# Max-pool subtract on one core: tiles of five rows in five slots, a loop by tile, and the last wait on SyncE

## The chip, the cores and the metric

One core of a Trainium2 chip; the other cores are idle. The metric is device time in microseconds (us), the median of several executions. All runs below were in the fast state: the clock that the chip granted, as a share of the full one, was 1.000. The "span" is the time from the first to the last instruction in a profile, some 1.8 us less than the device time. A transfer "lands" when its semaphore tells that all of it has arrived. A "row" is always the kernel's unit of 128 partitions x 8 KB = 1.049 MB. The kernel moves 128 rows in and 128 rows out.

## The reference

```python
# x: float32, B, C, H, W = 8, 64, 256, 256
x_r = x.reshape(B, C, 32, 8, 32, 8)
pooled = x_r.max(axis=(3, 5))
upsampled = np.repeat(np.repeat(pooled, 8, axis=2), 8, axis=3)
return x - upsampled
```

Each 8 x 8 window loses its own maximum. Every byte is read once and written once: 268.44 MB.

## The kernel before

SyncE issues the loads and ScalarE the stores. VectorE takes a tile's maxima in one reduce and subtracts them row by row, in place in the ring. TensorE only relays "loaded" semaphores into one counter. The tiles lie in the slots of a ring in on-chip memory. The first tile (the head) and the last (the tail) are worked in smaller pieces, of the rows that `HEAD` and `TAIL` list.

```python
HEAD = [2, 2]; SIZE = 4; ROUNDS = 5; TAIL = [2, 1, 1]; SLOTS = 6
ring = data.tile([P, SLOTS * SIZE * ROW], F32, name="ring")     # ROW = 2048 floats
# ... SyncE: a slot is loaded again when its store has landed
        if landed[slot]:
            nc.sync.wait_ge(stored[slot], 16 * landed[slot])
        nc.sync.dma_start(out=sbuf(i, lo, R), in_=dram(x_rows, i)[:, part])   # ...
# ... ScalarE
        nc.scalar.wait_ge(ready, done)
        nc.scalar.dma_start(out=dram(out_rows, i)[:, part], in_=sbuf(i, lo, R))   # ...
    nc.scalar.wait_ge(final, 16 * n_final)
# ... VectorE: the head, then
    with nc.vector.Fori(0, ROUNDS):
        with nc.vector.Fori(0, SLOTS) as slot:
            take(filled, 1)
            pool_and_subtract(ring[:, bass.ds(slot * (SIZE * ROW), SIZE * ROW)], ..., SIZE)
# ... then the tail
```

## Time and profile before

| | before |
|---|---|
| device time, first three runs | 627.47 us (627.42 to 627.50) |
| span in the profile | 625.5 us |
| VectorE busy | 562.6 us (90%) |
| the two DMA queues | 49.9% + 49.7% of 16 engines' span |
| period of a four-row tile | 19.36 us |
| last landing to end of span | 1.11 us |

A busy VectorE and a busy set of DMA engines stand side by side here. Which one bounds is read from who waits for whom.

### The profile page before, as it was taken

To read this page: it belongs to the slowest core of one execution; us is meant where nothing else is said; L and a number is where in the kernel's file an instruction comes from. 1 tells how busy PE (TensorE), PEld (TensorE's weight loads), DVE (VectorE), ACT (ScalarE), POOL (GpSimd) and SP (SyncE) were. 2 spreads that over 40 slices of the span, in tenths; PEclk is the share of its full clock that TensorE was granted. 3 is DMA by queue.
4 is the path that set the end of the run, shared out by engine and by line. 5 is a ranking of instruction groups with operands and counts; after the bars stand their busy time and mean duration, and the time that the engine had idled before them with its cause. 6 is when DMAs were issued, how large, how long until landed. Compare 5 with 4: busy or idle time off the path is not lost. (4 is left out here: it accounts for less than half of the span.)

```text
span 625.5 us, 613 instructions
## 1 busy us (share of the span) xinstructions
DVE 562.6 (90%) x163; POOL 0.2 (0%) x4
## 2 busy tenths in 40 slices
DVE  4999999998898888988889888898888998888983
POOL 0000000000000000000000000000000000000000
DMA  8999999999999999999999999999999999999998
GB/s 369 402 434 438 436 434 436 434 436 434 434 432 427 425 434 436 436 436 434 436 434 436 434 434 427 430 425 436 436 436 434 436 436 434 434 436 434 425 427 363
DMA packets 9792, 268.44 MB, mean 429 GB/s; under 512 B 1088, under 2 KB 1088, under 8 KB 1088
## 3 DMA queue, kind: packets, MB, share of 16 engines
q1 hardware_dynamic: 4752, 134.22, 49.9%
q10 hardware_dynamic: 5040, 134.22, 49.7%
HBM read 134.22 MB, written 134.22 MB: 429 GB/s over the span
## 5 line engine op out<-in xcount | busy, mean ns | idle before, releaser
L81 DVE TENSOR_REDUCE tops<-ring (+2 forms) x35 | 278.4, 7953 | 48.4 <-DVEq L75 48.4
L93 DVE TENSOR_TENSOR ring<-ring,tops (+1 forms) x128 | 285.0, 2287 | 5.2 <-DVEq L75 0.2
L164 POOL MEMSET const-bfloat16-1.0<- 128x1 bf16 x1 | 0.1, 102 | 0.0
L164 POOL MEMSET const-uint8-127<- 128x1 uint8 x1 | 0.1, 102 | 0.0
L164 POOL MEMSET const-float32-0.0<- 128x1 f32 x1 | 0.1, 99 | 0.2 <-issue 0.2
L164 POOL MEMSET const-float32-1.0<- 128x1 f32 x1 | 0.1, 99 | 0.0
## 6 DMA issues: line engine op xcount, KB each, us to landing
ring<-in_x_dram SPq DMA_DIRECT2D x31, 4096.0 KB, 62.1
out_dram<-ring ACTq DMA_DIRECT2D x30, 4096.0 KB, 35.9
out_dram<-ring ACTq DMA_DIRECT2D x3, 2048.0 KB, 19.3
ring<-in_x_dram SPq DMA_DIRECT2D x2, 2048.0 KB, 9.5
out_dram<-ring ACTq DMA_DIRECT2D x2, 1024.0 KB, 9.2
```

The lines of the kernel that those rows point to most:

```text
L81: nc.vector.tensor_reduce(out=maxs if R > 1 else maxs[:, 0], in_=(wins.rearrange("p r ph ow pw -> p r ow ph pw") if R > 1 else wins[:, 0]. ...
L93: sub = nc.vector.tensor_tensor(out=wins[:, r], in0=wins[:, r], in1=maxs[:, r].unsqueeze(1).unsqueeze(3).to_broadcast([P, pH, oW, pW]), op ...
L164: nc = _bacc.Bacc("TRN2", target_bir_lowering=False, num_devices=1)
```

## The change

The intent is fewer, larger transfers, a simpler loop and shorter waits around VectorE. The title of the change also names the head "in halves"; the head was `[2, 2]` before, so this changes nothing.

```diff
-HEAD = [2, 2]
-SIZE = 4
-ROUNDS = 5
+HEAD, HEAD_OUT = [2, 2], [2, 2]
+SIZE, TILES = 5, 24
 TAIL = [2, 1, 1]
-SLOTS = 6
+SLOTS = 5
...
-        ).then_inc(reduced, 1)
-        take(reduced, 1)
+        ).then_inc(reduced if nth is None else pooled, 1)   # pooled: head and tail, no decrement
...
-        nc.scalar.wait_ge(final, 16 * n_final)
+        nc.sync.wait_ge(final, 16 * n_final)
...
-        with nc.vector.Fori(0, ROUNDS):
-            with nc.vector.Fori(0, SLOTS) as slot:
-                take(filled, 1)
+        with nc.vector.Fori(0, TILES) as i:
+            slot = i % SLOTS
+            take(filled, 1)
...                                # head and tail wait on the load's semaphore directly
```

## The prediction

> **What bounds the kernel now.** I read the page first, beginning with its busy shares and the row of DMA shares:
>
> ```profile
> span 625.5 us, 613 instructions
> DVE 562.6 (90%) x163; POOL 0.2 (0%) x4
> ...
> DMA  8999999999999999999999999999999999999998
> ...
> DMA packets 9792, 268.44 MB, mean 429 GB/s; under 512 B 1088, under 2 KB 1088, under 8 KB 1088
> ...
> q1 hardware_dynamic: 4752, 134.22, 49.9%
> q10 hardware_dynamic: 5040, 134.22, 49.7%
> ```
>
> VectorE (DVE) works 90% of the span, but the DMA engines have no slice below eight tenths, and the packets of the load queue (q1) and the store queue (q10) fill 49.9% + 49.7% = 99.6% of what 16 engines have. Next the stretches: the first microseconds, the steady middle, the end.
>
> ```profile
> 2.00:3.00 1.00, 0.00 (x0) 0.00 (x0) 1.00 1.02 229
> 3.00:4.00 1.00, 0.00 (x0) 0.00 (x0) 1.00 0.93 393
> ...
> 100.00:590.00 490.00, 447.70 (x128) 0.00 (x0) 1.00 1.00 433
> ...
> 616.00:618.00 2.00, 0.21 (x1) 0.00 (x0) 1.00 1.05 451
> ...
> 620.00:622.00 2.00, 0.00 (x0) 0.00 (x0) 1.00 1.04 438
> ```
>
> The last two columns are DMA share and GB/s. From 100 to 590 us the share is 1.00; after VectorE's last instruction ends at 616.2 us the DMA still runs full until the last packet ends at 624.0 us (packet records). So the set of 16 engines is the bound from the first load to the last store. VectorE only waits for it, in the timeline and the waits:
>
> ```profile
> 539.94 8.69 DVE L81 TENSOR_REDUCE tops<-ring  x1 [1.64 <-DVEq L75]
> 548.78 8.90 DVE L93 TENSOR_TENSOR ring<-ring,tops  x4
> ...
> 559.30 8.69 DVE L81 TENSOR_REDUCE tops<-ring  x1 [1.62 <-DVEq L75]
> ...
> SPq L110 <- DMA out_dram<-ring: 522.6, 26, 47.2
> ```
>
> One tile takes 559.30 - 539.94 = 19.36 us, of which VectorE idles 1.6 us; SyncE (SP) waits for stores in order to reload a slot. Last, the issues:
>
> ```profile
> ring<-in_x_dram SPq DMA_DIRECT2D x31, 4096.0 KB, 62.1
> out_dram<-ring ACTq DMA_DIRECT2D x30, 4096.0 KB, 35.9
> ```
>
> A load lands 62.1 us after its issue, over three periods of 19.36, so some two more loads always stand queued behind it; a store lands after 35.9, so the store queue has a backlog of 35.9 - 19.4 = 16.5 us. Neither queue runs dry.
>
> **A ledger of the DMA time.** A row is one unit of 128 x 8 KB = 1.049 MB; the kernel moves 128 rows in and 128 out. The steady period is 19.362 us for 8 rows (landings of the load semaphores, 116.17 us for six tiles), 2.4203 us a row. 256 x 2.4203 = 619.6 us. The first packet starts at 1.93 us and the last ends at 624.01, which is 622.08, so about 2.5 us are lost besides; the slow first microseconds above (229 and 393 GB/s) are where, because at every later landing the count of rows moved lies the same 2.7 us behind. The remaining 1.9 us before the first packet and 1.5 us after the last are start, receipt and closing barriers.
>
> Of the 2.4203 us, how much hangs on packet size? The packet records have medians of 309 ns for 8192 B, 611 for 16384 and 1213 for 32768: doubling costs 302 and 602, so 7 to 9 ns are fixed. The period says somewhat less: 8 rows at 435.2 GB/s are 19.275 us, the measured excess is 0.087 us for 16 data packets on each engine, 5.4 ns each. So **5 to 8 ns a packet**.
>
> **What the Trainium skill says.** "DMA: Bandwidth & Descriptors", section "Specifications", gives a fabric ceiling of 435 GB/s for a core's 16 DMA engines; the trace agrees, 433 to 435 in the long windows, so there is at most half a per cent above this kernel. The same page, section "Why small descriptors are slow (HBM only)", states a fixed overhead of about 3 cycles per packet; the trace has 5 to 8 ns, more than 3 cycles of the 850 MHz that the page names, but of that kind. Its section "Queues, rings and completion order" says that each DMA engine round-robins between its queue rows at packet granularity. The trace agrees in a way that matters here: while the head is stored in 16 KB packets beside loads in 32 KB packets, stores get a third of the engines. From 36.88 to 51.48 us they moved 2 rows and loads 4. Its section "Latency and other measured facts" warns of HBM row pitches that are large powers of two; the old pitch (32 KB) shows no such loss here, and the new one (40 KB) is not a power of two.
>
> **The change, part by part.**
>
> *Larger tiles.* Thirty tiles of four rows become 24 of five: the loads go from 33 to 27, the stores from 35 to 29. Data packets: before, 7808 of 32 KB, 640 of 16 KB, 256 of 8 KB, in all 8704; after, 24 x 128 x 2 = 6144 of 40 KB, 128 of 32 KB for the last load, the same 640 and 256, in all 7168. That is 1536 fewer, and 12 x 16 = 192 fewer completion packets of 9 ns. Saved: 1536 x 5 to 8 ns / 16 = 0.48 to 0.77 us, plus 192 x 9 / 16 = 0.11 us. **About 0.6 us.** All of this is on the path, because the DMA engines never idle.
>
> *VectorE.* A four-row reduce takes 8.686 us and a two-row one 4.42, so 2.13 a row: five rows 10.82. Five subtractions at 8.90 / 4 = 2.225 are 11.13. With the 0.15 us gap a tile needs 22.1 us against a DMA period of 10 x 2.418 = 24.18, so it still waits about 2 us a tile. Its busy total stays near 562 us. The loop's new remainder (slot from tile number) is one register operation; those of the old loop take 0.05 to 0.1 us and stand between landing and reduce, off the path. The waits taken directly instead of through TensorE's relay, and without the decrement, shorten a landing-to-reduce time of 0.3 us at the head and tail. That is off the path too.
>
> *Five slots.* The ring holds 25 rows instead of 24, but after the head only four tiles, still 24 rows, are loaded ahead. With 40 KB load packets beside 16 KB head stores, stores get 2/7 of the engines: 4 rows stored while 10 are loaded. At 21.2 us, where stores begin, 7.2 rows are loaded; so 17.2 are loaded when the head is out, at 4.6 + 21.2 x 2.42 = 56 us (before: 51.5 us, with 15.5 loaded). From there the queues alternate evenly and loads stay 13.2 rows ahead of stores (before about 11). Then a load waits in line (24 - 17.2 + 5) x 4.84 = 57 us, and a store lands 13.2 x 4.84 - 22.4 = 41 us after its issue. Both exceed the 24.2 us of a transfer; no queue runs dry. The same working gives 62 and 35 for before, which matches the page's 62.1 and 35.9.
>
> *The end.* When the last load lands, some 12 rows are still to be stored, 12 x 2.42 = 29 us. VectorE is done with the second last tile about then and with the last (2, 1 and 1 rows) 19 us later, eight before the last row must be there. So the end is still the draining of the store queue.
>
> *SyncE in place of ScalarE for the last wait.* Before: the last landing at 624.37, ScalarE's branch at 624.39, its drain at 624.54, SyncE's closing instruction at 624.58. After, one hop between engines goes, but SyncE's two closing waits, done early before, come after the last landing; they stand 0.06 us apart. Net 0, give or take 0.1 us.
>
> Sum: 627.47 - 0.6 = **626.9 us**.
>
> **Rivals.** (1) *VectorE becomes the bound*, if five-row tiles run slower than their shape says. For: only 2.1 us a tile of slack. Against: the forms scale evenly from one to two to four rows (2.28, 4.42, 8.69), and the subtractions don't change. A tile at 25 us would make 24 x 0.8 = 19 us more, 646. Very unlikely. (2) *The 40 KB runs are cut into two packets each*, or go slower. Nothing in the profile has one above 32 KB. A cut would make 6144 more packets, up to 6144 x 8 / 16 = 3.1 us more than my count: 629 to 630. Unlikely, and still inside 2%. (3) *Coarser slots starve a queue*: a load can be issued only once five rows are out. Against: the ledger's lines of 57 and 41 us. If it happened once a tile for 1 us, 24 us more. (4) *No gain at all*: the small excess over 435.2 GB/s goes with bytes[...], not packets; then 627.4. This is the strongest rival, since the two ways to get the packet's cost differ by half. (5) *More gain than mine*: were the 9 ns of packet overhead fully serial, 1 us; 626.4.
>
> **Range and chances.** Rivals 4 and 5 give 627.4 and 626.4; the three runs before lie within 0.08 us, and the closing hop adds 0.1. A little more on the slow side for rival 2 gives 626.1 to 628.0. Two per cent is 12.5 us; a gain of that is above the fabric ceiling (614.9 us would be less than 268.44 MB at 435.2 GB/s, 616.8). A loss of it needs rival 1 or 3: 2%.
>
> **What the new profile would show.** Right: 7168 data and 896 completion packets, 8064 in all; DMA slices still at nine; a tile period of 24.18 us; five-row reduces of 10.8 us; VectorE idle near 2 us a tile before the reduce; loads landing after about 57 us and stores after about 41; the second store landing at 56 us; the DMA full until about 1.5 us before the end. Wrong: more than 8100 packets (rival 2), a period above 24.2, DMA slices of eight in the middle (rival 3), VectorE idle near zero (rival 1), or a period of 24.20, which is exactly 1.25 times the old (rival 4).

## The result

The changed kernel took 626.98 us (626.82 to 627.02, 6 runs) against 627.49 us (627.36 to 627.79, 6 runs): ratio 0.9991, 95% interval 0.9978 to 1.0004. A ratio is the mean time of one kernel's fast runs over that of the other's of the same rounds, so not quite the ratio of these medians. In a later set of rounds it took 626.94 us against 627.18.

The page of the changed kernel, the same lines as were shown of the one before:

```profile
span 625.2 us, 557 instructions
DVE 561.1 (90%) x157; POOL 0.2 (0%) x4
...
DMA  9999999999999999999999999999999999999998
...
DMA packets 8065, 268.44 MB, mean 429 GB/s; under 512 B 897, under 2 KB 897, under 8 KB 897
...
q1 hardware_dynamic: 3888, 134.22, 49.9%
q10 hardware_dynamic: 4176, 134.22, 49.7%
```

The queues hold 3888 + 4176 = 8064 packets in place of 9792, and still fill 99.6% of the engines. The views that follow are the middle stretch (DMA share and GB/s last), the timeline of VectorE (start, duration, and in brackets the idle time before), SyncE's waits (total us, times, longest) and the issues (size, median us from issue to landing):

```profile
100.00:590.00 490.00, 449.14 (x124) 0.00 (x0) 1.00 1.00 434
```

```profile
548.92 10.82 DVE L81 TENSOR_REDUCE tops<-ring  x1 [2.08 <-DVEq L75]
559.89 11.10 DVE L96 TENSOR_TENSOR ring<-ring,tops  x5 [0.15 <-DVEq L75]
573.09 10.82 DVE L81 TENSOR_REDUCE tops<-ring  x1 [2.10 <-DVEq L75]
```

```profile
SPq L113 <- DMA out_dram<-ring: 612.8, 22, 84.2
```

```profile
ring<-in_x_dram SPq DMA_DIRECT2D x24, 5120.0 KB, 57.6
out_dram<-ring ACTq DMA_DIRECT2D x24, 5120.0 KB, 40.8
```

A tile of five rows takes 573.09 - 548.92 = 24.17 us, with VectorE idle for 2.1 us of it. The DMA engines are still the bound, and the 434 GB/s are barely above the 433 of before. For differences this small the rate must be read finer. The packet records give us per row moved between 100 and 590 us: 2.4203 before, 2.4183 after. Over the 240 rows of the 24 tiles that is 240 x 0.0020 = 0.48 us. The window from the first packet to the last shrank from 622.08 to 621.44 us, by 0.64.

The span fell by less: 625.48 to 625.21, by 0.27. Of the rest, 0.25 us were lost after the last landing, where 1.11 us became 1.37. The other 0.12 lie before the first packet (1.93 and 1.95 us) and between the end of the last packet and its landing (0.36 and 0.46 us).

### The profile page after: what moved, and what is told of

The parts are those of the page before. It is cut to its first block, busy times and chain, and to the rows that moved or that the text cites. A ratio compares the mean times of both kernels' runs of the same rounds, so it can differ in the third digit from the quotient of the medians.

```text
span 625.2 us, 557 instructions
## 1 busy us (share of the span) xinstructions
DVE 561.1 (90%) x157; POOL 0.2 (0%) x4
## 3 DMA queue, kind: packets, MB, share of 16 engines
q1 hardware_dynamic: 3888, 134.22, 49.9%
q10 hardware_dynamic: 4176, 134.22, 49.7%
## 6 DMA issues: line engine op xcount, KB each, us to landing
ring<-in_x_dram SPq DMA_DIRECT2D x24, 5120.0 KB, 57.6
out_dram<-ring ACTq DMA_DIRECT2D x24, 5120.0 KB, 40.8
```

## The experiments

Twelve runs were made. Ten change the changed kernel by the edit shown; two run the kernels before and after again as they are.

### Is the longer end SyncE's wait?

```diff
-        nc.sync.wait_ge(final, 16 * n_final)
+        nc.scalar.wait_ge(final, 16 * n_final)
```

> The changed kernel with the wait for the last stores back on ScalarE, all else kept. Theory (SyncE's wait delays the closing barrier: 1.37 us from the last landing to the end of the span against 1.11 before): the landing-to-end time falls to 1.1 us and the kernel to about 626.7 us, 0.27 less than the changed one. Rival (the longer end is something else, such as the five slots or the loop): it stays at 1.37 us, 627.0 us.

Measured: 626.73 us (626.69 to 626.82) against 627.11 for the kernel before. From the last landing to the end it took 1.10 us. So the longer end is SyncE's wait. It was repeated beside the changed kernel on one chip, the latter also being run again as it is:

> The changed kernel with ScalarE's last wait, on the same chip as the changed kernel. Theory: 0.25 us under the changed kernel, 626.7 us, from landing to end 1.1 us in place of 1.37, and with that the fastest of all. Rival (the first run of it was lower by chance): the same as the changed kernel.

> The changed kernel once more, on one chip with the next two and with more runs of the kernel before: in a repeat of itself against itself the kernel before moved by 0.3 us, so its first 0.5 us of gain is not settled. If the gain is 24 five-row tiles' fewer packets less a longer end (0.64 us of DMA window saved, 0.27 us lost at the end), it is 627.0 us and 0.1 to 0.5 us under the kernel before.

Measured: 626.70 us (626.62 to 626.87) with ScalarE's wait, 626.94 (626.88 to 626.96) for the changed kernel, 627.18 (627.04 to 627.97) for the kernel before. The ends were 1.10 and 1.37 us. Every one of the five runs with ScalarE's wait lies below every one of the five without it, and all of these below all nine runs of the kernel before. This is the fastest version found (against the kernel before, ratio 0.9993, interval 0.9979 to 1.0006): differences this small show in the separate ranges and in the trace.

How SyncE's wait lengthens the end shows in the trace's instruction records (start, engine, what it is). The last store landed at 624.37 us before and at 623.84 after:

```
before                                     after
624.387 Scalar  branch after the wait      623.859 Sync    branch after the wait
624.543 Scalar  drain, signals SyncE       624.014 Sync    signals the others
624.576 Sync    closing instruction        624.052 Scalar  drain, 624.058 Vector, 624.059 Tensor
                                           624.184 Sync    waits for VectorE
                                           624.248 Sync    waits for TensorE and itself
                                           624.314 Sync    closing instruction
```

SyncE gathers the engines at the end. The drains of the others wait for a signal that SyncE gives only after its own work. Before, SyncE had given it long ago and only waited for ScalarE, which its waits show. First the kernel before, then the one with ScalarE's wait; columns are total us, times, longest:

```profile
SPq L101 <- ACTq L101: 8.2, 1, 8.2
```

```profile
SPq L104 <- ACTq L104: 10.8, 1, 10.8
```

The changed kernel has no such line. When SyncE itself is last, the signal goes out to three engines and comes back: 0.47 us from landing to closing instruction against 0.21. The difference is the 0.26 us.

### Is the gain the packet size, or the loop and the waits?

Two runs keep the new loop and waits but return to four rows in six slots, once with SyncE's last wait and once with ScalarE's; one runs the kernel before against itself. The diff is the edit of the first; the second also has ScalarE's wait, as above.

```diff
-SIZE, TILES = 5, 24
+SIZE, TILES = 4, 30
-SLOTS = 5
+SLOTS = 6
```

> The changed kernel with tiles of four rows in six slots, 30 of them; new loop, new waits and SyncE's last wait kept. Theory (all of the gain is the number of DMA packets): 8704 data packets again, 2.4203 us a row moved in the middle as before the change, and with the later end of 1.37 us about 627.75 us, 0.25 over the kernel before. Rival (the loop and the directly taken waits bring the gain): 627.0 us or less.

> Tiles of four rows in six slots with the new loop and the directly taken waits, and ScalarE's last wait: only the loop and the waits differ from the kernel before. The same with SyncE's last wait took 628.3 us, 0.5 more than the sum of the parts. Theory (loop and waits are off the path): as the kernel before, 627.1 to 627.5 us. Rival (the new loop costs something with four rows): 628.0 us.

> The kernel before against itself, for the size of the noise: 627.5 us, ratio 1.000. Any ratio off by 0.0003 or more would mean that the 0.5 us between the two kernels is near the noise. Its single runs also show whether the span of 625.5 us in the first profile is typical, since the time fell by 0.5 us but the span of the profile only by 0.3.

Measured: with SyncE's wait 628.31 us (627.82 to 628.46), more than the 627.75 expected. With ScalarE's wait 627.27 (627.11 to 627.99), where the kernel before took 627.18. The kernel before against itself: 627.38 (627.07 to 627.92) against 627.11, ratio 1.0002. The rates in the middle were 2.4207, 2.4204 and 2.4205 us a row. All four profiles with four rows lie between 2.4203 and 2.4207, and all profiles of DMA-bound five-row kernels with whole transfers and four or five slots between 2.4183 and 2.4184. The rate goes with the tile, not with the loop or the waits, whose share of the time is within the noise.

That noise has a form. Single runs of four-row kernels scatter by 0.4 to 0.9 us within a set of rounds, those of the five-row kernels with five slots and whole transfers by at most 0.25. In the profiles the last landing of a four-row kernel comes at 624.37 or 624.38, or else at 625.03 or 625.04. In the two late ones the last of the 16 DMA engines is 0.53 and 0.76 us behind the others, and 0.24 and 0.19 in the early ones. So part of the 628.31 is a late engine, as its one profile shows. Why all five of its executions were slow was not found.

### Does the cost really go with the number of packets?

The same five-row tiles, slots and VectorE work, but each load and each store of a tile goes as five transfers of one row.

```diff
-            for k, (lo, R) in enumerate(cuts(HEAD if i == 0 else [sizes[i]])):
+            for k, (lo, R) in enumerate(cuts(HEAD if i == 0 else [1] * sizes[i])):
...                     # the same for the stores; waits count five landings a tile
```

> The changed kernel, same tiles, slots and VectorE work, but each load and store of a five-row tile goes as five transfers of one row: 8 KB packets, and a completion packet for each transfer and engine. Theory (4.9 ns a packet): 9 packets a row on each engine in place of 1.8, 7.2 x 4.9 = 35 ns a row, 2.4535 us a row, 8.5 us over 240 rows: 635.4 us. Rival (the small excess over the fabric's rate goes with bytes): 627 us. Rival (tile count or slots brought the gain): 627 us too, since neither changes.

Measured: 636.99 us (636.53 to 637.36). Its packets and its middle stretch:

```profile
DMA packets 36146, 268.47 MB, mean 422 GB/s; under 512 B 4016, under 2 KB 4016, under 8 KB 4016
```

```profile
100.00:590.00 490.00, 448.87 (x123) 0.00 (x0) 1.00 1.01 427
```

The DMA share is full, and yet the rate is 427 GB/s in place of 434. A row took 2.4537 us against 2.4535 expected. That is (2.4537 - 2.4183) / 7.2 = 4.9 ns for each packet on each engine, and both rivals fall. (The four- and five-row kernels give 0.0020 / 0.45 = 4.4 ns with rates of four digits; 4.9 comes from the larger difference.) One thing is not separated: 9, 2.25 and 1.8 packets a row are 9 divided by the rows of a transfer, and data packets, completion packets and transfers grow by the same factor in these runs. The 4.9 ns are thus an average over data and completion packets, and a cost of the transfer itself would look the same.

The whole time is 1.6 us above the estimate. In the profiled run (637.36 us) one DMA engine finished at 634.17 us and the other fifteen by 632.45; that lag of 1.7 us, where the changed kernel has 0.5, is most of it.

### Would larger packets gain more?

Six rows a tile in four slots, 48 KB a packet, with ScalarE's last wait:

```diff
-SIZE, TILES = 5, 24
+SIZE, TILES = 6, 20
-SLOTS = 5
+SLOTS = 4
```

> Twenty tiles of six rows in four slots (48 KB a packet) with ScalarE's last wait. Theory (4.9 ns for each data or completion packet on an engine, from the two kernels' 2.4203 and 2.4183 us a row): 2.4168 us a row, 0.4 us less than the changed kernel over 240 rows, and 0.27 less at the end: 626.3 us. Rival (five rows are already past what packet size gives, or four slots starve a queue): 626.7 us or more.

Measured: 629.52 us; four runs lie between 629.46 and 629.55, one at 627.39. This is a miss. The last stretches of its profile:

```profile
620.00:622.00 2.00, 0.00 (x0) 0.00 (x0) 1.00 0.99 418
622.00:624.00 2.00, 0.00 (x0) 0.00 (x0) 1.00 0.28 119
624.00:626.00 2.00, 0.00 (x0) 0.00 (x0) 1.00 0.06 25
```

A share of 0.06 is one engine of sixteen (1/16 = 0.0625): fifteen ended by 624.23 us, one at 626.68. In the packet records 35 load packets between 118 and 558 us take 30 to 800 ns more than the others; the DMA-bound five-row kernels with five slots and whole transfers have no such load packet, or one, after the first 25 us. The middle rate was 2.4189 us a row, not 2.4168. The slow packets account for that: their excess is 6.6 us, or 0.41 us on each of 16 engines, and 0.0021 us over the 203 rows between 100 and 590 us is 0.43. The median packet, 1815 ns, is 301 above the 1514 of 40 KB, the same step as from 32 to 40 KB. Four slots, or 48 KB packets? The next run tells.

### How many slots are needed?

Five-row tiles in four and in three slots (`SLOTS = 4`, `SLOTS = 3`).

> The changed kernel with four slots of five rows. Theory (the count of rows): a load still finds 1.8 rows of earlier loads, some 9 us, ahead of it when a slot comes free, so the load queue does not run dry; a load lands some 33 us after its issue in place of 57.6; time 627.0 us. Rival (coarse slots starve a queue): some us a tile, 640 us or more. It also tells why six rows in four slots had 2.5 us of lag on one DMA engine at the end: if the four slots did that, it comes here too (629 us, slow load packets all through); if the 48 KB packets did, it does not.

> The changed kernel with three slots. Theory: a slot's round is now a load, 22.5 us of VectorE and a store, 24 + 22.5 + 24 and some 5 us of latencies, 76 us for three tiles, 25.3 us a tile against 24.2: DMA slices below nine and some 645 us (630 to 650). Rival (the DMA engines are the bound whatever the slots): 627 us.

Measured with four slots: 626.94 us (626.85 to 627.20), a rate of 2.4184 us a row, last engine 0.66 us behind. Its loads:

```profile
ring<-in_x_dram SPq DMA_DIRECT2D x24, 5120.0 KB, 33.4
```

The landing takes 33.4 us, as counted. So the fifth slot is not needed for the time, and four slots alone don't delay an engine by 2.5 us. What it was in the six-row kernel, the 48 KB packets or the tile of six rows with them, stays open.

With three slots: 663.62 us (662.48 to 667.47), above the expected range.

```profile
span 660.7 us, 557 instructions
...
DMA  9999999999999999999999999999999999999998
...
DMA packets 8064, 268.44 MB, mean 406 GB/s; under 512 B 896, under 2 KB 896, under 8 KB 896
```

Now the queues run dry, and the DMA share does not show it: every slice but the last is still at nine. It was expected to fall. Instead the packets themselves take longer, a 40 KB load packet 1593 ns on average in place of 1518, a store packet 1553 in place of 1514. No load packet ran from 251.3 to 259.1 us, for example; with five slots a queue never paused for over 2.7 us between 100 and 590. Many of the long packets stand where a queue starts again: after a load issued at 200.3 us, 15 store packets that began between 204 and 205 us took 2318 ns on average. GB/s tells what the share hides.

### How much slack has VectorE?

Extra subtractions of 128 x 1024 on unrelated memory, between landing and reduce of every five-row tile; the results stay correct.

```diff
             take(filled, 1)
+            for _ in range(4):          # or 1
+                flat = zero.to_broadcast([P, 1024])
+                nc.vector.tensor_tensor(out=spare, in0=flat, in1=flat, op=subtract).then_inc(reduced, 1)
+                take(reduced, 1)
```

> One extra subtraction a tile in place of four, 1.34 us with its wait by the run with four, 32 us of VectorE work in all. Theory: it goes into the 2.1 us of idle time before each reduce, 627.0 us, VectorE busy 94 to 95%. Rival (VectorE's work is on the path in part, as its 90% would let one think): up to 32 us more, 659 us.

> The changed kernel with four extra subtractions of 128 x 1024 on unrelated memory per five-row tile, between landing and reduce, some 1.3 us each with their wait. Theory (VectorE has 2.1 us of slack a tile): a tile costs VectorE 27.3 us, VectorE becomes the bound from the first tile on, 26 + 24 x 27.3 + 18 and some 8 at the end and outside the span: about 707 us. Rival (VectorE's time is hidden further, by backlog): clearly less.

Measured with one: 626.89 us (626.83 to 626.92). With four: 720.02 us (719.96 to 720.08). VectorE's busy time with one, and the timeline with four:

```profile
DVE 589.3 (94%) x182; POOL 0.2 (0%) x4
```

```profile
310.95 10.82 DVE L83 TENSOR_REDUCE tops<-ring  x1 [0.40 <-DVEq L77]
321.93 11.10 DVE L98 TENSOR_TENSOR ring<-ring,tops  x5 [0.15 <-DVEq L77]
332.94 5.34 DVE L149 TENSOR_TENSOR spare<-zero 128x1024 f32<-128x1024 f32 x4
338.68 10.82 DVE L83 TENSOR_REDUCE tops<-ring  x1 [0.40 <-DVEq L77]
```

Twenty-eight us more of VectorE work (589.3 - 561.1) cost nothing. With four, a tile takes 338.68 - 310.95 = 27.73 us, and 24 of them are 666 us. Here VectorE is the bound. The estimate had 27.3 a tile: each extra instruction costs 1.34 us with its wait, and one gap of 0.4 us before the reduce was not counted. Over 24 tiles that is 10 of the 13 us by which the estimate fell short.

## Why the prediction was right, and where not

**The bound.** Right. The DMA engines are full in both kernels; VectorE's extra work is hidden up to its 2.1 us a tile and shows in full beyond.

**Larger tiles, about 0.6 us.** Right in mechanism and nearly in size. The packets came out at 8064 as counted. The rate in the middle fell by 0.0020 us a row, 0.48 us over the tiles, completion packets included. The prediction's 5 to 8 ns a packet were 4.9, measured with one-row transfers, so its range lay too high. Its own terms add up to 0.59 to 0.88 us, of which it took the low end, 0.6. Rival 4, no gain because the excess goes with bytes, falls with that run. A period of 24.18 us was told, and 10 x 2.4183 is 24.18.

**VectorE.** Right: reduces of 10.82 us, an idle time of 2.1 us, a busy total of 561.1. The change's "shorter waits" came true at the first piece alone, where landing to reduce fell from 0.23 to 0.02 us; in the loop it grew from 0.37 to 0.48, by the new loop's register work. Both are off the path.

**Five slots.** Right: loads landed after 57.6 us (57 told), stores after 40.8 (41), the head's second store at 55.3 (56). Rival 3, coarse slots, came true with three slots and not with four or five.

**SyncE for the last wait.** This step failed: "Net 0, give or take 0.1 us" was 0.26 us longer. The listing of instructions showed SyncE's two closing waits; that the other engines' drains hang on a signal of SyncE's was not followed, so a round trip was taken for a hop saved.

**The ledger of lost time.** Wrong in place, not in sum. The 2.5 us were put in "the slow first microseconds". By the packet records about 0.9 us are lost there after the first packet. Another 0.8 is lost between 19 and 24 us, around the first store (issued at 17.6 us, first packet at 21.2), when load packets take up to 1.1 us longer; and 0.7 at the end, where the engines finish one after another: the DMA was not full "until the last packet ends", its share was 0.28 from 623 to 624 us. The change kept all three nearly as they were, so the sum held.

**The total.** 626.9 told, 626.98 and 626.94 measured. The gain told was 0.6 us. Measured it was 0.51 in one set of rounds and 0.24 in another, as the kernel before itself moved. The sum in the profile is 0.64 us of DMA window less 0.25 at the end and 0.12 at the other edges, 0.27. By the parts, 0.48 us for the tiles less 0.26 for the wait leaves some 0.2. That the first number was met so closely was in part luck: the base was on the high side, 627.47 in the first runs and 627.11 to 627.18 in the later ones, and this hid the longer end.

## What to carry to other kernels

When the DMA engines are full from the first load to the last store, count packets and bytes: here neither the new loop nor VectorE's waits nor the fifth slot changed the time beyond noise, as long as neither queue ran dry. A count of rows in the ring told in advance that four slots suffice and three do not, though not how much three cost. Put the last wait on an engine other than the one that gathers the others at the end, here on ScalarE and not on SyncE (0.26 us). And read GB/s beside the DMA share, because in the middle of these kernels a DMA share of 0.98 to 1.01 went with 434, 427 or 407 GB/s, depending on packet size and on dry queues.

## What the Trainium skill lacked or had wrong

- "DMA: Bandwidth & Descriptors", section "Why small descriptors are slow (HBM only)", gives some 3 cycles a packet. Here it was 4.9 ns for each packet, from runs with 8 KB and 40 KB packets; at the 850 MHz that the page names for the fabric that is 4.2 cycles. The page does not say which clock its cycles are of, and the 4.9 ns include completion packets.
- The same page, section "Where 436 GB/s comes from", says that the HBM side, about 358 GB/s, binds for transfers between HBM and SBUF. It does not say there that this is the share of a core whose neighbour works too; the page's section "Measured" does. With one core working, loads and stores together ran at 433 to 434 GB/s here.
- No page read has the closing round trip: a wait of SyncE's for the last DMA costs 0.26 us more than the same wait on ScalarE (1.37 against 1.10 us from the last landing to the end).
- None has the loss seen around the start of a second queue beside a running one: load packets up to 1.1 us longer between 19 and 24 us, 0.8 us of the whole. Its cause was not tested.
- None gives, for transfers issued from SyncE and ScalarE, a size for the single engine that comes in behind the others: 0.2 to 0.8 us with 32 and 40 KB packets, 1.7 us with one-row transfers, 2.5 us with 48 KB packets. Its cause was not found here.
